# A list of waiting instructions per engine behind a planner, in a one-core hybrid attention and state-space layer

## The chip, the core and the metric

The kernel runs as one program on one core of a Trainium2 chip. A core has a matrix engine (PE, with its weight loads shown as PEld), a vector engine (DVE), a scalar engine (ACT), a general engine (POOL) and a sync engine (SP) that issues most transfers. Each engine works through its own list of instructions in the order in which the program wrote them; an instruction that waits for another engine holds all that stand behind it on its own engine. The metric is the device time of one execution in microseconds (us), the median of several runs.

## What is computed

One layer for 1024 positions of width 2048 in float32: a combined input projection, sparse attention in half of the width, a Mamba-2 state-space mixer in the other half, an output projection and a LayerNorm on the residual.

```
u = einsum('bsd,de->bse', h, w_in)
q, k, v, z_attn, q_idx, k_idx, w_idx, z_ssd, xbc, dt_raw = split(u)
o_attn = dsa_attention(rope(q), rope(k), v, rope(q_idx), rope(k_idx), w_idx) * silu(z_attn)
o_ssd  = ssd_mixer(xbc, z_ssd, dt_raw, ...)
sub = einsum('bse,ed->bsd', concat(o_attn, o_ssd), w_out)
h = layer_norm(alpha * h + sub)
```

In the attention an indexer scores all admissible keys of a query, the 256 best are kept, and softmax attention with 8 query heads over 2 key heads runs on these.

## The kernel before

**Arithmetic.** The two projections run in blocks of 128 by 128 by 512. Each float32 operand is split into a high part and a rest, and three products are added: high by high, high by rest, rest by high. Most of the weight is handled in a Strassen-like scheme of seven products over sums of blocks. Names in the profile: `wr` is a raw piece of weight (128x512), `wh` its high part made by ACT, `wl` the rest made by DVE or POOL; `xh` and `xl` are the same for the activations; `pj`, `a` and `o` are PSUM banks; `u` is the general SBUF tile; `s` (program name `s4`) a wider one; `sm` small columns; `mx`, `pt`, `o_sc` and the like are scratch in DRAM. One piece of weight feeds twelve matmuls of the input projection.

**Stages, roughly.** The span begins with plain projections and the indexer's scores of the first half of the rows (0 to 215 us), goes on with products of the Strassen scheme among state-space and attention work (to 1350 us, with the top-256 search by bisection on ACT and DVE from about 600 us on), and ends with the output projection (from 1350 us) and the LayerNorm.

**What sets the order.** `Layer.run` walks through the pieces of the projections in a fixed order and writes out their matmuls. Between them `Flow.pump` advances some hundred tasks (Python generators such as `t_w` for splitting one piece of weight, `t_x` for an activation, `t_ssd`, `t_attn`, `t_topk`), the first in the list of priorities that is `ready`. What ready means is decided by a model, class `Sim`: it keeps a clock for each engine, a cost for each operation, the times at which data are written, and the port that DVE and POOL share. Every operation passes through `Engine.__getattr__`: it is written into the program at once (`f(*args, **kw)`), and `Sim.run` then advances the model's clocks. So the program's order on each engine is the order in which the planner took the steps, and where two steps interleave badly, an engine waits in that order. `Flow.new` hands out a tile from a numbered slot; the tile framework makes the first user of the new tile wait for the users of the old one.

All work is issued from one line (L346, the call in `Engine.__getattr__`), so rows of the profile tell operations apart by tile names. Rows of the order carry two numbers on a name: the first is the kernel's own count of tiles and is the same before and after, the second is the framework's.

Of the kernel before, what the change touches and what calls it, by code (L numbers as in the profile page):

```python
# [12 lines left out]
AF = mybir.ActivationFunctionType  # L13
ALU = mybir.AluOpType

D = 2048
# [108 lines left out]
class Port:  # L125
# [3 lines left out]
    def __init__(self):  # L129
        self.busy = []  # L130
# [26 lines left out]
def in_dram(x):  # L157
    return "DRAM" in str(x.space)
# [6 lines left out]
class Sim:  # L165


    LAT = 70.0

    def __init__(self):  # L170
        self.clk = dict(PE=0.0, V=0.0, A=0.0, G=0.0, SP=0.0, AQ=0.0, D=0.0)
        self.slot = {}
        self.port = Port()
        self.table = None
        self.recent = []

    @staticmethod
    def region(x):
# [34 lines left out]
    def note(self, notes, end, eng):  # L213
        for s, p0, p1, a, b, w in notes:
            inside = lambda e: e[0] >= p0 and e[1] <= p1 and e[2] >= a and e[3] <= b
            s[2] = [e for e in s[2] if not (inside(e) and (w or (not e[4] and e[6] == eng)))]
            s[2].append((p0, p1, a, b, w, end, eng))

    def last(self, tile):
# [67 lines left out]
    def run(self, eng, op, outs, ins, kw):  # L287

        if op == "dma_start":
            return self.dma(eng, outs[0], ins[0])  # L290
        n = outs[0].free_size()
        at, notes = self.deps(outs, ins, eng)
        busy, took = self.cost(eng, op, outs, ins, kw, n)
        if eng == "A":
            kind = {AF.Silu: "silu", AF.Exp: "exp", AF.Ln: "ln"}.get(kw.get("func"))
            if kind and kind != self.table:
                self.table = kind
                self.clk["A"] += 1283
# [17 lines left out]
        cell = [start + took, start]  # L316
        if eng == "V":
            self.recent = self.recent[-24:] + [cell]
        self.note(notes, cell, eng)
        return cell  # L320

    def dma(self, eng, out, in_):
        q = {"SP": "SP", "A": "AQ", "G": "G"}[eng]
        at, notes = self.deps([out], [in_], "D")
        start = max(self.clk[q], at)
        self.clk[q] = start + (900.0 if eng == "G" else 400.0)
        sb = in_ if in_dram(out) else out
        row = max(sb.ap[-1][1] * 4, 64)
        x = max(start + 400, self.clk["D"])
        self.clk["D"] = x + max(out.size(), in_.size()) * 4 * (1 / 352 + 0.35 / row) * (2.0 if eng == "G" else 1.2 if in_dram(out) and in_dram(in_) else 1.0)  # L330
        cell = [self.clk["D"] + (2000.0 if eng == "G" else 3400.0), start]
        self.note(notes, cell, "D")
        return cell


class Engine:
# [5 lines left out]
    def __getattr__(self, op):  # L342
        f = getattr(self.engine, op)

        def call(*args, **kw):
            f(*args, **kw)  # L346
            is_ap = lambda x: hasattr(x, "tensor") and hasattr(x, "ap")
            outs = [x for x in args[:1] if is_ap(x)] + [kw[k] for k in ("out", "accum_out") if is_ap(kw.get(k))]
            ins = [x for x in args[1:] if is_ap(x)] + [x for k, x in kw.items() if is_ap(x) and k not in ("out", "accum_out")]
            if op == "tensor_tensor_reduce":  # L350
                outs.append(ins.pop())
            if op == "activation" and len(args) > 2:
                kw["func"] = args[2]
            self.flow.placed(self.flow.sim.run(self.name, op, outs, ins, kw))
        return call


# [6 lines left out]
class Event:  # L364
# [5 lines left out]
    @property  # L370
    def t(self):
        return max(c[0] for c in self.cells) if self.cells else None
# [15 lines left out]
class Flow:  # L388
# [6 lines left out]

    def __init__(self, nc):
        self.sim = Sim()
        self.nc = Engines(self, nc)
# [12 lines left out]
    @property  # L411
    def t(self):
        return self.sim.clk["PE"]

    def placed(self, cell):
        self.steps += 1
        self.last = cell
        self.cells.append(cell)
# [8 lines left out]
    def new(self, tag, shape, dtype=F):  # L427

        free = self.slots[tag]
        assert free, ("no slot", tag)  # L430
        slot = min(free)
        free.remove(slot)
        self.n += 1
        home, i = slot[1]
        t = self.pool[home].tile(shape, dtype, name=f"{home}_{self.n}", tag=f"{home}{i}")
        self.where[t.tensor.name] = (tag, slot[1])
        if tag == "u" and self.mixing:
            self.mixed.add(t.tensor.name)
        return t
# [153 lines left out]
class Layer:  # L593
# [316 lines left out]
    def run(self):  # L910
        fl = self.fl
# [1298 lines left out]
```

## Time and profile before

| | |
|---|---|
| median of 3 runs | 1756.56 us (1754.19 to 1759.01) |
| the profiled execution's own time | 1756.95 us |
| its span, first to last instruction | 1754.8 us |
| PE busy | 1642.7 us, 94% |
| DVE busy | 1353.6 us, 77% |
| ACT busy | 985.3 us, 56% |
| POOL busy | 259.9 us, 15% |
| mean granted clock of PE | 0.98 |
| DMA | 431.67 MB, 246 GB/s |

The profile shows one execution. A matmul's duration in it covers its way through the array, and the next one starts before it ends; the pace is read from the starts. Idle time in front of an instruction stands in brackets in the timeline, with what ended it.

### The profile page before, as it was taken

What the parts mean: (1) busy time and instruction counts of PE and PEld (TensorE: products, weight loads), DVE (VectorE), ACT (ScalarE), POOL (GpSimd) and SP (SyncE); (2) the same over time, 40 slices, a digit from 0 to 9 for tenths busy, and PEclk for the clock granted to TensorE, in tenths of its full rate; (3) what the DMA queues carried; (4) which work ended last, traced back from release to release, by engine and by line L of the source; (5) the groups of instructions that cost most, each with busy time, mean ns of one, the idle gap of its engine ahead of it and who ended that gap; (6) DMA issues with size and microseconds to landing.
All of it is one profiled execution on the core that took longest, in us unless ns stands there. A gap on an engine that the chain in (4) does not pass through costs nothing.

```text
span 1754.8 us, 26174 instructions
## 1 busy us (share of the span) xinstructions
PE 1642.7 (94%) x7989; PEld 1344.5 (77%) x7989; DVE 1353.6 (77%) x2991; ACT 985.3 (56%) x1920; POOL 259.9 (15%) x321
## 2 busy tenths in 40 slices
PE   7999999999999899899899999989999889999993
PEld 6888878777777678787677788878788778778782
DVE  6897465568898878888966677898886778888875
ACT  6657766655665498988732456547555434323351
POOL 2200021001112100002131322002111000100122
PEclk9999999999999999999999999999999999999997
DMA  8599888596377688989899897886565997777998
GB/s 290 170 308 349 233 262 230 144 314 156 86 240 214 198 248 277 324 251 294 284 273 313 253 300 193 249 293 203 190 200 173 315 296 242 228 211 237 332 267 199
DMA packets 272685, 431.67 MB, mean 246 GB/s; under 512 B 29600, under 2 KB 87328, under 8 KB 272032
## 3 DMA queue, kind: packets, MB, share of 16 engines
q1 hardware_dynamic: 259872, 406.93, 70.6%
q0 software_dynamic: 12672, 23.07, 8.9%
q8 instruction: 63, 1.03, 0.2%
q14 instruction: 78, 0.64, 0.1%
HBM read 338.56 MB, written 131.17 MB: 268 GB/s over the span
## 4 chain that ended last, share of the span: by engine, by line
PE 53%; DVE 19%; DMA 14%; ACT 6%; issue 5%; SPq 2%; POOL 1%; DVEq 0%; POOLq 0%; ACTq 0%
PE pj L346 40%; DVE u L346 9%; PE a L346 8%; PE o L346 5%; DVE wl L346 3%; ACT u L346 3%; DMA wr<-wt 2%; DMA u<-mx 2%; DVE s L346 2%; DVE xl L346 2%; SPq L346 2%; DVE wr L346 2%; DMA u<-xt 1%; ACT wh L346 1%; DMA u<-arow 1%
## 5 line engine op out<-in xcount | busy, mean ns | idle before, releaser
L346 PE MATMUL pj<-xh,wh 128*128 128x512 f32 (+1 forms) x1520 | 595.7, 392 | 30.1 <-ACT wh L346 26.7
L346 PE MATMUL pj<-xh,wl 128*128 128x512 f32 (+1 forms) x1520 | 586.1, 386 | 19.8 <-DVE wl L346 19.5
L346 PE MATMUL pj<-xl,wh 128*128 128x512 f32 (+1 forms) x1520 | 583.8, 384 | 0.9 <-POOL xl L346 0.6
L346 ACT ACTIVATE wh<-wr 128x512 fp32r<-128x512 f32 (+1 forms) x488 | 298.7, 623 | 283.0 <-PE pj L346 118.8
L346 DVE TENSOR_TENSOR wl<-wr,wh 128x512 fp32r<-128x512 f32 (+1 forms) x456 | 311.3, 693 | 148.2 <-ACT wh L346 145.9
L346 PEld LDWEIGHTS pj<-xh,wh 128*128 128x128 f32 x1520 | 288.1, 190 | 88.7 <-ACT wh L346 32.9
L346 PEld LDWEIGHTS pj<-xh,wl 128*128 128x128 f32 x1520 | 287.8, 189 | 88.0 <-DVE wl L346 32.1
L346 PEld LDWEIGHTS pj<-xl,wh 128*128 128x128 f32 x1520 | 288.6, 190 | 52.2 <-POOL xl L346 1.3
L346 PE MATMUL a<-u,u 128*128 128x512 f32 (+3 forms) x776 | 176.5, 351 | 3.7 <-ACT u L346 1.3
L346 DVE TENSOR_TENSOR u<-u,u 128x512 f32<-128x512 f32 (+6 forms) x240 | 147.3, 626 | 14.3 <-ACT u L346 10.4
L346 PEld LDWEIGHTS a<-u,u 128*128 128x128 f32 x776 | 127.2, 190 | 37.5 <-DVE s L346 9.1
L346 ACT ACTIVATE u<-u 128x512 f32<-128x512 f32 (+4 forms) x209 | 116.1, 576 | 62.3 <-DVE u L346 42.2
L346 ACT ACTIVATE u<-a 128x256 fp32r<-128x256 f32 (+3 forms) x182 | 61.3, 364 | 149.3 <-PE a L346 72.1
L346 ACT ACTIVATE u<-s,sm 128x1024 bf16<-128x1024 f32 (+7 forms) x132 | 129.7, 983 | 19.2 <-DVE sm L346 17.3
L346 PE MATMUL pj<-wh,xh 128*128 128x512 f32 x310 | 128.4, 414 | 4.6 <-ACT xh L346 3.8
L346 DVE TENSOR_TENSOR xl<-u,xh 128x512 fp32r<-128x512 f32 (+1 forms) x168 | 111.1, 693 | 27.9 <-ACT xh L346 27.4
L346 ACT ACTIVATE xh<-u 128x512 fp32r<-128x512 f32 (+1 forms) x184 | 102.4, 586 | 47.6 <-DVE u L346 18.5
L346 DVE TENSOR_TENSOR wr<-wr,wr 128x512 f32<-128x512 f32 x160 | 114.9, 719 | 14.7 <-DMA wr<-wt 11.7
L346 PE MATMUL pj<-wl,xh 128*128 128x512 f32 x310 | 122.9, 396 | 1.1 <-DVE wl L346 1.1
L346 PE MATMUL pj<-wh,xl 128*128 128x512 f32 x310 | 123.0, 397 | 0.9 <-DVE xl L346 0.9
L346 POOL DMA_DIRECT2D o<-wo x64 | 53.1, 843 | 458.9 <-DMA o<-wo 250.4
L346 ACT ACTIVATE a<-a 128x512 f32<-128x512 f32 (+3 forms) x160 | 76.2, 505 | 71.4 <-PE a L346 69.1
(164 smaller groups left out, 2065.3 us busy)
## 6 DMA issues: line engine op xcount, KB each, us to landing
wr<-wt SPq DMA_DIRECT2D x424, 256.0 KB, 5.1
u<-xt SPq DMA_DIRECT2D x80, 256.0 KB, 5.9
u<-mx SPq DMA_DIRECT2D x72, 256.0 KB, 5.5
o<-wo POOLq DMA_DIRECT2D x64, 256.0 KB, 6.5
u<-x SPq DMA_DIRECT2D x64, 256.0 KB, 5.3
wr<-o SPq DMA_DIRECT2D x64, 256.0 KB, 5.0
pt<-u SPq DMA_DIRECT2D x48, 256.0 KB, 3.2
u<-pt SPq DMA_DIRECT2D x48, 256.0 KB, 4.8
```

The source lines that it names most:

```text
L346: f(*args, **kw)
```

## The change

Instructions are no longer written into the program when they are planned. `Engine.__getattr__` now makes a closure `go` and hands it to the new `Flow.call`. That runs the planner's model as before (`Sim.run`, so every decision of the planner is the same), collects the instructions on which the new one depends by its data (`Sim.before`), gives it a cost, and puts it into a list for its engine. The new class `Queue` has clocks of its own and writes the instructions out. Its `step` looks at the first 12 (PE), 10 (DVE, ACT, POOL) or 8 (SP) of each list, takes of each engine the oldest one that is ready when the engine is free, or else the one that will be ready first, and writes out the earliest over all engines. It is run only as far as is needed: `Flow.new` runs it until all users of the slot's old tile are written out, and the end of `Layer.run` empties it. Matmuls into one PSUM tile keep their order, and ACT's functions that need a table keep theirs. This second model has no shared port of DVE and POOL; its transfer time is 4000 ns on SP's queue where the planner's is 3400.

With lists of length one the program on each engine is, row by row, the one before. As it is, 7,450 of 7,675 PE instructions are written out when they are the oldest of their list, 2,009 of 2,869 on DVE, 1,176 of 1,609 on ACT, 292 of 317 on POOL and 1,213 of 1,738 on SP (counted in the program, as are the next numbers). Of 488 splits `wh` on ACT 183 stand earlier among ACT's instructions than before, by 2.3 places on average, and 69 later by 1.7; of 456 splits `wl` on DVE 145 earlier by 2.3 and 96 later by 2.2. Of 184 `xh` on ACT 24 stand earlier and 71 later by 3.1; of 168 `xl` on DVE 18 earlier and 66 later by 3.8. The 49 table loads stay 49.

```diff
     def note(self, notes, end, eng):
...
-            s[2] = [e for e in s[2] if not (inside(e) and (w or (not e[4] and e[6] == eng)))]
+            s[2] = [e for e in s[2] if not (inside(e) and (w or (not e[4] and e[6] == eng and e[5] is not end and e[5][2].end is not None)))]
...
+    def before(self, eng, outs, ins):
+
+        recs, floor = [], 0.0
+        for w, xs in ((False, ins), (True, outs)):
+            for x in xs:
+                k, name, p0, p1, a, b = self.region(x)
+                floor = max(floor, self.floor.get(name, 0.0))
+                s = self.slot.get(k)
+                if s is not None and s[0] == name:
+                    recs += [e[5][2] for e in s[2] if (e[4] or w) and (e[2] < b and a < e[3] and e[0] < p1 and p0 < e[1]
+                                                                       or w and e[6] == eng == "PE")]
+        return recs, floor
...
+class Queue:
...
+    WIN = dict(PE=12, V=10, A=10, G=10, SP=8)
+    LAND = 4000.0
+    LAT = 75.0
...
+    def step(self):
+        best = None
+        for e, q in self.pend.items():
+            free = self.clk[e]
+            if best and free >= best[0]:
+                continue
+            for i, c in enumerate(q[:self.WIN[e]]):
+                at = c.floor
+                for r in c.recs:
+                    if r.end is None:
+                        break
+                    t = r.end + (0.0 if r.eng == e and not r.size else self.LAT) if not r.eng == e == "PE" else 0.0
+                    if t > at:
+                        at = t
+                else:
+                    at = max(at, free)
+                    if best is None or at < best[0]:
+                        best = at, e, i
+                    if at == free:
+                        break
+        at, e, i = best
+        c = self.pend[e].pop(i)
+        c.go()
...
         def call(*args, **kw):
-            f(*args, **kw)
+            go = lambda: f(*args, **given)
+            given = dict(kw)
...
-            self.flow.placed(self.flow.sim.run(self.name, op, outs, ins, kw))
+            self.flow.call(self.name, op, outs, ins, kw, go)
...
+        old = self.sim.users(self.keys.get((home, i)))
+        self.queue.until(old)
         t = self.pool[home].tile(shape, dtype, name=f"{home}_{self.n}", tag=f"{home}{i}")
...
         fl.drain()
+        fl.queue.flush()
```

Two places show what moves. The first is on ACT at about 602 to 612 us of the span. `wh_1328` and its neighbours are high parts of weight, `u_1323<-a_1338` is a copy of the state-space mixer, the rows with 128x640 and 128x1024 are steps of the top-256 search. Before:

```order
L346 ACTIVATE wh_1336_6795<-wr_1249_6367 128x512
L346 ACTIVATE u_1323_6735<-a_1338_6812 128x128
L346 ACTIVATE wh_1339_6819<-wr_1268_6472 128x512
L346 ACTIVATE u_1317_6716,sm_1316_6715<-s4_949_4988,sm_1316_6715 128x640
L346 ACTIVATE u_1317_6716,sm_1316_6715<-s4_952_4991,sm_1316_6715 128x1024
L346 ACTIVATE wh_1328_6742<-wr_1292_6582 128x512
L346 ACTIVATE u_1335_6791,sm_1334_6790<-s4_950_4989,sm_1334_6790 128x768
```

With the change, on the same engine at the same place:

```order
L441 ACTIVATE wh_1336_6777<-wr_1249_6355 128x512
L441 ACTIVATE wh_1328_6724<-wr_1292_6566 128x512
L441 ACTIVATE wh_1339_6798<-wr_1268_6461 128x512
L441 ACTIVATE u_1323_6689<-a_1338_6780 128x128
L441 ACTIVATE u_1323_6689<-a_1346_6808 128x128
L441 ACTIVATE wh_1332_6749<-wr_1306_6654 128x512
L441 ACTIVATE u_1317_6683,sm_1316_6682<-s4_949_4976,sm_1316_6682 128x640
```

`wh_1328` and `wh_1339` have moved in front of the copy, and the two long search steps behind it.

The second place is SP's list at about 1357 to 1366 us, at the start of the output projection: `u_3087<-mx1_6` and `u_3098<-mx1_7` load activations that become `xh` and `xl`, the other `mx` loads are for later products. Before:

```order
L346 DMA u_3087_14913<-mx1_6_284 128x512
L346 DMA u_3088_14918<-hst2_296 128x256
...
L346 DMA u_3095_14928<-arow1_299 128x512
L346 DMA u_3098_14933<-mx1_7_285 128x512
L346 DMA u_3103_14947<-mx1_0_278 128x512
L346 DMA u_3104_14949<-mx0_0_262 128x512
L346 DMA u_3107_14953<-mx1_1_279 128x512
L346 DMA u_3108_14955<-mx0_1_263 128x512
```

With the change:

```order
L441 DMA u_3088_14904<-hst2_217 128x256
...
L441 DMA u_3095_14911<-arow1_220 128x512
L441 DMA u_3103_14945<-mx1_0_199 128x512
L441 DMA u_3104_14946<-mx0_0_183 128x512
L441 DMA u_3107_14949<-mx1_1_200 128x512
L441 DMA u_3108_14950<-mx0_1_184 128x512
L441 DMA u_3087_14903<-mx1_6_205 128x512
L441 DMA u_3098_14914<-mx1_7_206 128x512
```

Four `mx` loads that were behind the two now stand in front of them, and `u_3087` has also gone behind the loads of the state-space step.

## Rows read from the trace of the kernel before

**Rows 1.** The head of the page: the span, and busy time, share and instructions of PE and DVE.

```profile
span 1754.8 us, 26174 instructions
PE 1642.7 (94%) x7989; PEld 1344.5 (77%) x7989; DVE 1353.6 (77%) x2991; ACT 985.3 (56%) x1920; POOL 259.9 (15%) x321
```

**Rows 2.** Busy time by stretch of the span: start:end, length, busy us of PE, PEld, DVE, ACT and POOL (with counts), granted clock of PE, share of DMA, GB/s.

```profile
0.00:50.00 50.00, 40.18 (x237) 33.08 (x238) 34.10 (x71) 28.79 (x65) 13.06 (x25) 0.97 0.87 284
50.00:600.00 550.00, 535.65 (x2563) 438.25 (x2562) 406.86 (x947) 337.87 (x693) 82.89 (x105) 0.99 0.74 224
600.00:900.00 300.00, 275.36 (x1238) 220.52 (x1237) 246.62 (x609) 245.11 (x478) 34.91 (x38) 0.97 0.88 277
900.00:1350.00 450.00, 435.50 (x2210) 362.42 (x2208) 348.82 (x737) 234.91 (x440) 84.28 (x103) 1.00 0.77 239
1350.00:1704.00 354.00, 335.62 (x1661) 273.72 (x1660) 285.31 (x572) 131.21 (x236) 28.45 (x30) 0.98 0.83 264
1704.00:1755.00 51.00, 20.34 (x90) 16.52 (x88) 31.92 (x58) 7.45 (x10) 16.36 (x20) 0.74 0.88 200
```

**Rows 3.** Who PE waited for over the whole span: us in total, times, longest.

```profile
PE pj L346 <- ACT wh L346: 26.7, 11, 8.0
PE pj L346 <- DVE wl L346: 20.6, 23, 4.2
...
PE pj L346 <- ACT xh L346: 5.1, 4, 2.1
```

**Rows 4.** PE's timeline at the longest of these waits: start us, us, operation, count, and in brackets the idle time before it and what ended it.

```profile
612.47 0.80 PE L346 MATMUL pj<-xh,wh 128*128 128x512 f32 x1 [7.96 <-ACT wh L346]
613.06 0.63 PE L346 MATMUL pj<-xl,wh 128*128 128x512 f32 x1
613.49 0.63 PE L346 MATMUL pj<-xh,wl 128*128 128x512 f32 x1
...
616.69 0.39 PE L346 MATMUL pj<-xh,wh 128*128 128x512 f32 x1
616.91 0.39 PE L346 MATMUL pj<-xl,wh 128*128 128x512 f32 x1
```

**Rows 5.** ACT's timeline in the ten microseconds before that matmul, same columns.

```profile
602.03 0.62 ACT L346 ACTIVATE wh<-wr 128x512 fp32r<-128x512 f32 x1
609.02 0.28 ACT L346 ACTIVATE u<-a 128x128 f32<-128x128 f32 x1 [6.37 <-DVE u L346]
609.20 0.62 ACT L346 ACTIVATE wh<-wr 128x512 fp32r<-128x512 f32 x1
609.72 0.82 ACT L346 ACTIVATE u<-s,sm 128x640 bf16<-128x640 int16 x1
...
610.66 1.15 ACT L346 ACTIVATE u<-s,sm 128x1024 bf16<-128x1024 int16 x1
...
611.80 0.61 ACT L346 ACTIVATE wh<-wr 128x512 fp32r<-128x512 f32 x1
```

**Rows 6.** Waits in PE's timeline at seven other places, same columns.

```profile
25.54 0.51 PE L346 MATMUL pj<-xh,wh 128*128 128x256 f32 x1 [3.07 <-ACT wh L346]
...
315.61 1.26 PE L346 MATMUL o<-u,u 128*128 128x256 f32 x3 [2.32 <-ACT u L346]
...
630.04 0.50 PE L346 MATMUL pj<-xh,wh 128*128 128x512 f32 x1 [1.15 <-ACT wh L346]
...
643.76 0.50 PE L346 MATMUL pj<-xh,wh 128*128 128x512 f32 x1 [1.27 <-ACT wh L346]
...
859.72 0.50 PE L346 MATMUL pj<-xh,wh 128*128 128x512 f32 x1 [2.39 <-ACT wh L346]
...
892.37 0.50 PE L346 MATMUL pj<-xh,wh 128*128 128x512 f32 x1 [1.26 <-ACT wh L346]
...
975.04 0.50 PE L346 MATMUL pj<-xh,wh 128*128 128x512 f32 x1 [1.91 <-ACT wh L346]
```

**Rows 7.** Waits in PE's timeline at six more places, same columns.

```profile
740.90 0.79 PE L346 MATMUL pj<-xh,wh 128*128 128x512 f32 x1 [4.49 <-ACT wh L346]
...
1173.58 0.50 PE L346 MATMUL pj<-xh,wh 128*128 128x512 f32 x1 [2.24 <-ACT wh L346]
...
1274.56 0.51 PE L346 MATMUL pj<-xh,wl 128*128 128x512 f32 x1 [4.18 <-DVE wl L346]
...
1365.11 0.50 PE L346 MATMUL pj<-wh,xh 128*128 128x512 f32 x1 [1.69 <-ACT xh L346]
...
1369.32 0.50 PE L346 MATMUL pj<-wh,xh 128*128 128x512 f32 x1 [2.14 <-ACT xh L346]
...
1547.65 0.68 PE L346 MATMUL a<-o,u 128*128 128x1 f32 x4 [3.17 <-DVE u L346]
```

**Rows 8.** SP's timeline at the second place: when it issues the `mx` loads.

```profile
1357.17 0.38 SPq L346 DMA_DIRECT2D u<-mx  x1
...
1363.07 2.85 SPq L346 DMA_DIRECT2D u<-mx  x5
```

**Rows 9.** Who DVE waited for longest over the whole span: us in total, times, longest.

```profile
DVE wl L346 <- ACT wh L346: 145.9, 109, 4.3
```

**Rows 10.** DVE's timeline at one of its longest splits.

```profile
1435.57 1.34 DVE L346 TENSOR_TENSOR wl<-wr,wh 128x512 fp32r<-128x512 f32 x1 [1.44 <-ACT wh L346]
1436.84 0.68 DVE L346 TENSOR_TENSOR s<-o,s 128x512 f32<-128x512 f32 x1
```

**Rows 11.** POOL's timeline at the same time.

```profile
1435.10 1.27 POOL L346 TENSOR_TENSOR xl<-u,xh 128x512 fp32r<-128x512 f32 x1 [11.70 <-ACT xh L346]
```

More of the change, by code (lines that the diff above doesn't have):

```diff
@@ L175, in __init__ @@
         self.recent = []
+        self.floor = {}
     @staticmethod
@@ L215, in note, with users @@
             inside = lambda e: e[0] >= p0 and e[1] <= p1 and e[2] >= a and e[3] <= b
-            s[2] = [e for e in s[2] if not (inside(e) and (w or (not e[4] and e[6] == eng)))]
+            s[2] = [e for e in s[2] if not (inside(e) and (w or (not e[4] and e[6] == eng and e[5] is not end and e[5][2].end is not None)))]
             s[2].append((p0, p1, a, b, w, end, eng))
+    def before(self, eng, outs, ins):
[9 more added lines that the diff above has]
+        return recs, floor
+    def users(self, key):
+        s = self.slot.get(key)
+        return [e[5][2] for e in s[2]] if s else []
     def last(self, tile):
@@ L315, in run @@
         self.clk[eng] = start + busy
-        cell = [start + took, start]
+        cell = [start + took, start, None]
         if eng == "V":
@@ L330, in dma, with __init__, put, done @@
         self.clk["D"] = x + max(out.size(), in_.size()) * 4 * (1 / 352 + 0.35 / row) * (2.0 if eng == "G" else 1.2 if in_dram(out) and in_dram(in_) else 1.0)
-        cell = [self.clk["D"] + (2000.0 if eng == "G" else 3400.0), start]
+        cell = [self.clk["D"] + (2000.0 if eng == "G" else 3400.0), start, None]
         self.note(notes, cell, "D")
         return cell
+class Call:
+    __slots__ = ("eng", "go", "recs", "floor", "busy", "took", "size", "table", "end", "cell")
+class Queue:
+    WIN = dict(PE=12, V=10, A=10, G=10, SP=8)
+    LAND = 4000.0
+    LAT = 75.0
+    def __init__(self):
+        self.pend = {e: [] for e in self.WIN}
+        self.clk = {e: 0.0 for e in self.WIN}
+        self.bus = 0.0
+        self.table = self.tabled = None
+    def put(self, c):
+        c.end = None
+        if c.table:
+            if self.tabled is not None:
+                c.recs.append(self.tabled)
+            self.tabled = c
+        self.pend[c.eng].append(c)
+    def step(self):
[21 more added lines that the diff above has]
+        c.go()
+        self.done(c)
+        if c.size:
+            x = max(at + 400, self.bus)
+            self.bus = x + c.size
+            self.clk[e] = at + c.busy
+            c.end = self.bus + (self.LAND if e == "SP" else self.LAND + 500)
+        else:
+            if c.table and c.table != self.table:
+                self.table = c.table
+                at += 1283
+            self.clk[e] = at + c.busy
+            c.end = at + c.took
+        c.go = c.recs = None
+    def done(self, c):
+        pass
+    def until(self, cs):
+        for c in cs:
+            while c.end is None:
+                self.step()
+    def flush(self):
+        while any(self.pend.values()):
+            self.step()
@@ L397, in __init__ @@
         self.sim = Sim()
+        self.queue = Queue()
+        self.keys = {}
         self.nc = Engines(self, nc)
@@ L413, in t, with call @@
         return self.sim.clk["PE"]
+    def call(self, eng, op, outs, ins, kw, go):
+        sim = self.sim
+        c = Call()
+        c.eng, c.go, c.table, c.size = eng, go, None, 0.0
+        c.recs, c.floor = sim.before(eng, outs, ins)
+        if op == "dma_start":
+            d = sim.clk["D"]
+            cell = sim.run(eng, op, outs, ins, kw)
+            sb = ins[0] if in_dram(outs[0]) else outs[0]
+            row = max(sb.ap[-1][1] * 4, 64)
+            c.size = max(outs[0].size(), ins[0].size()) * 4 * (1 / 352 + 0.35 / row) * (
+                2.0 if eng == "G" else 1.2 if in_dram(outs[0]) and in_dram(ins[0]) else 1.0)
+            c.busy, c.took = (900.0 if eng == "G" else 440.0), 0.0
+        else:
+            c.busy, c.took = sim.cost(eng, op, outs, ins, kw, outs[0].free_size())
+            if eng in "VA":
+                c.busy, c.took = c.busy + 20.0, c.took + 20.0
+            if eng == "A":
+                c.table = {AF.Silu: "silu", AF.Exp: "exp", AF.Ln: "ln"}.get(kw.get("func"))
+            cell = sim.run(eng, op, outs, ins, kw)
+        cell[2] = c
+        c.cell = cell
+        self.queue.put(c)
+        self.placed(cell)
     def placed(self, cell):
@@ L434, in new @@
         home, i = slot[1]
+        old = self.sim.users(self.keys.get((home, i)))
+        self.queue.until(old)
         t = self.pool[home].tile(shape, dtype, name=f"{home}_{self.n}", tag=f"{home}{i}")
+        self.keys[home, i] = getattr(t.tensor, "tag", None) or t.tensor.name
+        if old:
+            self.sim.floor[t.tensor.name] = max(c.end + Queue.LAT for c in old)
         self.where[t.tensor.name] = (tag, slot[1])
```

## Prediction, made before the changed kernel was run

> **What bounds the kernel now.** I read the head of the page first. PE is busy 94% of the span, DVE 77% [rows 1]: PE is the bound, and a change that leaves its work alone can only win from the time in which it waits. The table by stretches says how much that is: in the middle, from 50 to 1704 us, PE is busy 535.65 + 275.36 + 435.50 + 335.62 = 1582.1 of 1654 us [rows 2], so 71.9 us are idle. Head and tail hold 9.8 and 30.7 us more; there PE waits for the first loads and for the LayerNorm after the last product, and the order within a list can do little for either. The worst middle stretch is 600 to 900 us, with 24.6 us idle of 300 and ACT busy 245 us.
>
> Next the waits of PE. ACT's high parts of weight `wh` end 26.7 us of them in 11 waits, DVE's rests `wl` 20.6 us in 23, the activations `xh` 5.1 us in 4 [rows 3]. Then why ACT is late. At the longest wait PE stands 7.96 us until 612.47 us [rows 4]. ACT was not short of time: it finished a split at 602.65 us, stood idle 6.37 us at a small copy that waited for DVE, and then took one split and two search steps before the split PE needed, at 611.80 us [rows 5]. Idle and held work together make the wait: a queue blocked at its head. DVE shows the same in small: 145.9 us of its idle time over the span are `wl` waiting for `wh`, in 109 waits of 1.3 us on average [rows 9], with other work behind them.
>
> **The change, part by part.** No matmul, split, transfer or table load is added or removed; a different writer puts the same instructions into the lists. So the sum has no term for work, only for waits that go, waits that come, and the clock.
>
> Waits on ACT that go. In the new order `wh_1328` stands ahead of the blocked copy and the two steps: nothing that held it remains in front except splits of 0.62 us [rows 5]. I count the whole 7.96 us [rows 4]. At the seven other places the instruction PE waits for has also moved in front of what was blocked or working ahead of it on ACT, and by enough to cover the wait or nearly so: 3.07 + 2.32 + 1.15 + 1.27 + 2.39 + 1.26 + 1.91 = 13.4 us [rows 6]. Together 21.3 us.
>
> Waits that stay. At 740.90, 1274.56 and 1547.65 us nothing that matters moves ahead of the late instruction: 4.49 + 4.18 + 3.17 = 11.8 us are left where they are [rows 7].
>
> Waits for DVE's `wl`. Of the 20.6 us [rows 3] about a third by place has its `wl` moved forward, usually past one instruction that is itself 0.68 us long [rows 10]. Bounds: nothing, if the `wh` in front of it is what is late, and 20.6 us, if all of them go. I take 7 us, a third, because the order shows 145 of 456 splits forward.
>
> The clock. After the 7.96 us wait the matmuls start 0.43 us apart, later 0.22 us [rows 4]: the granted clock is at the lower of its levels (1.2 GHz) until it returns to 2.4 GHz, after PE had stood still. From 613.06 to about 616.2 us some seven intervals lose 0.2 us each, 1.4 us. Bounds for all the waits that go: nothing, as after a short one, and as much again per us of wait as here, 1.4 / 7.96 x 28 = 5 us. I take 2 us, since most are short.
>
> Waits that come. On SP's list the loads that become `xh` for 1365.11 and 1369.32 us move behind four other `mx` loads. Five such issues took 2.85 us [rows 8], 0.57 us each, so both are issued about 4 x 0.57 = 2.3 us later. PE waits there already, 1.69 and 2.14 us [rows 7], so this is on its path. But the second load was followed closely by the four, and the same four feed the next products; I charge 2.3 us once. At 1173.58 us the split that PE waits for (2.24 us [rows 7]) has another instruction put in front: 1 us. Elsewhere 69 `wh` move back by 1.7 places and 96 `wl` by 2.2, an instruction there lasting 0.6 to 0.7 us [rows 5, 10]. Their bounds: nothing, if the pieces split ahead and the idle slots filled by the move cover them all, and 69 x 1.7 x 0.62 + 96 x 2.2 x 0.68 = 216 us, if none is covered. Rows that bear on it: of some 944 splits, 34 waits of PE are seen now [rows 3], one in 28; so of 165 moved back some six should be seen, at about 1.4 us each: 8 us. Together 11.3, say 12 us.
>
> SP's queue, 1,738 issues of about 0.4 us [rows 8], puts loads past stores that wait for data; I count that as nothing, hidden by the pieces loaded ahead, since PE's longest waits name splits and not transfers. PE's own order changes in few places, and matmuls of other banks then fill a wait; that is within the 7 us. Tail: DVE's and POOL's last lists keep the same work with swaps of neighbours; nothing.
>
> Sum against the profiled execution: 1756.95 - 21.3 - 7 - 2 + 12 = 1738.65. That execution lies 0.4 us above the median of the three runs, which changes nothing: 1739 us, 1.0% faster.
>
> One thing speaks against trusting the second model. It has no port shared by DVE and POOL. A split of DVE that lasts 0.68 us elsewhere took 1.34 us at 1435.57 us [rows 10] while POOL worked from 1435.10 for 1.27 us [rows 11]. The Trainium skill (SBUF — State Buffer, "Who interferes with whom") says that a DVE instruction with two SBUF inputs contends with a POOL instruction that reads SBUF, and that whichever issues second blocks for the other's whole length; the trace agrees with it here (0.66 us longer). By that rule the new order may put DVE work against POOL's that the planner's model kept apart. Going by rows alone, 0.66 us at each of the 25 places where POOL takes one out of turn would be 16 us of DVE time; DVE is idle 23% [rows 1], so I add nothing to the sum, and leave it to the range.
>
> **The rivals.** *Larger gain.* Filled idle slots add up: what ACT and DVE do in a slot they waste now is not in the way later, so backlogs shrink well beyond the places named. For it speaks that DVE alone wastes 145.9 us at splits [rows 9]; against it that PE can use no more than 71.9 us, and that it is busy 96.8% in 900 to 1350 us, where there is little to win. Half of the idle time gone and 4 us of clock: 1756.95 - 36 - 4 = 1717 us.
>
> *No effect.* PE waits for whichever operand comes last; as one split gets earlier the next one is late, and the 28 us come back at other pieces. For it: the four late activations and the places of rows 7 stay. Time: 1756.95 +/- 5.
>
> *Slower.* The second model takes from each list what it believes ready, and so pays for a fuller engine with the urgent work that was next. The activations are where this bites: 71 of 184 `xh` and 66 of 168 `xl` go back, by 3.1 and 3.8 places, about 2.1 us at 0.62 us a place. PE waits little for `xh` now (5.1 us [rows 3]), so there is room; but if that room is used up, 137 x 2.1 = 288 us of delay are there to be seen. The loss passes the gross gain of 30 us once one in ten of these is seen by PE. At one in six: 48 us, with the gain of 30: 1756.95 + 48 - 30 = 1775 us. It would lie in the stretches with many new activations, 1350 to 1704 us above all. Against it: SP issues many of their loads earlier.
>
> *It doesn't do what it says.* The new order is real on DVE, ACT and SP, as the counts show, but on PE 7,450 of 7,675 keep their turn; this case gives the time of no effect and is counted there.
>
> **How the numbers follow.** A measurement of this kernel can tell about 0.3% from no change, 5.3 us, so faster means below 1751.3. The forecast gets 0.47 (own range 1726 to 1750), the larger gain 0.18, no effect 0.13, slower 0.22. Faster: 0.47 + 0.18 = 0.65; same 0.13; slower 0.22. For 8 in 10 the low end reaches past the larger gain's 1717 to 1712, and the high end to 1768, which leaves out the worst part of the slower case.
>
> **What would show it.** Right: at about 600 us no ACT wait of six microseconds in front of the small copy and PE's wait of 8 us gone; PE's waits for `wh` down from 26.7 to about 8 us, those for `wl` to about 14; DVE's idle at `wl` for `wh` far below 145.9 us; PE's busy time in the middle about unchanged while the middle is some 18 us shorter. Wrong in size: the table by stretches with 600 to 900 us still at 275 of 300. Wrong in sign: waits of PE for `xh` or `xl` of over 25 us, or DVE instructions next to POOL's grown long by tens of microseconds in sum.

## The result, and the profile after

| | before | with the change |
|---|---|---|
| median | 1757.01 us (1754.19 to 1759.01) | 1680.84 us (1679.39 to 1681.48) |
| ratio | | 0.9566 [0.955, 0.9583] |
| span | 1754.8 us | 1677.6 us |

The change gains 4.3%, 76 us. The prediction had the sign and missed the size: 1739 us was forecast, and the range ended at 1712.

The head of the page after, which answers to [rows 1]:

```profile
span 1677.6 us, 26207 instructions
PE 1613.9 (96%) x7989; PEld 1342.0 (80%) x7989; DVE 1345.1 (80%) x2991; ACT 985.6 (59%) x1920; POOL 273.9 (16%) x321
```

The span is 77.2 us shorter. PE's idle time fell from 1754.8 - 1642.7 = 112.1 to 1677.6 - 1613.9 = 63.7 us, which gives 48.4. The other 28.8 us are busy time, with the same 7,989 matmuls. So PE's busy time before also held time that was lost; the part on the prediction takes it apart.

The table by stretches after, for [rows 2]; the columns are the same:

```profile
0.00:50.00 50.00, 44.95 (x270) 38.64 (x271) 38.58 (x77) 31.30 (x69) 13.38 (x26) 0.93 0.89 295
50.00:1650.00 1600.00, 1568.61 (x7721) 1303.39 (x7720) 1291.84 (x2889) 951.22 (x1847) 252.24 (x287) 1.00 0.83 257
1650.00:1678.00 28.00, 0.30 (x2) 0.00 (x0) 14.67 (x26) 3.04 (x4) 8.30 (x10) 0.56 0.85 183
```

In the middle 31.4 of 1600 us are idle, against 71.9 of 1654. Even the first 50 us hold 4.8 us more of PE's work.

Who waited for whom after, over the whole span (us, times, longest), for [rows 3] and [rows 9]:

```profile
DVE wl L441 <- ACT wh L441: 113.1, 108, 3.9
...
PE pj L441 <- DVE wl L441: 10.3, 13, 3.0
...
PE pj L441 <- ACT wh L441: 5.1, 2, 5.0
...
PE pj L441 <- ACT xh L441: 4.6, 2, 3.4
```

PE's waits for `wh` fell from 26.7 to 5.1 us, those for `wl` from 20.6 to 10.3, and DVE's for `wh` from 145.9 to 113.1.

The same place as [rows 4] and [rows 5], now near 582 us. ACT's timeline after:

```profile
579.62 0.63 ACT L441 ACTIVATE wh<-wr 128x512 fp32r<-128x512 f32 x1 [0.36 <-DVE wr L441]
581.35 0.63 ACT L441 ACTIVATE wh<-wr 128x512 fp32r<-128x512 f32 x1 [1.09 <-PE pj L441]
581.90 0.28 ACT L441 ACTIVATE u<-a 128x128 f32<-128x128 f32 x1
582.70 0.28 ACT L441 ACTIVATE u<-a 128x128 f32<-128x128 f32 x1 [0.52 <-PE a L441]
582.88 0.62 ACT L441 ACTIVATE wh<-wr 128x512 fp32r<-128x512 f32 x1
583.39 0.82 ACT L441 ACTIVATE u<-s,sm 128x640 bf16<-128x640 int16 x1
```

PE's timeline after, same place:

```profile
585.61 0.80 PE L441 MATMUL pj<-xh,wl 128*128 128x512 f32 x1 [2.95 <-DVE wl L441]
586.21 0.63 PE L441 MATMUL pj<-xh,wh 128*128 128x512 f32 x1
586.63 0.63 PE L441 MATMUL pj<-xl,wh 128*128 128x512 f32 x1
```

DVE's timeline after, same place:

```profile
583.01 0.68 DVE L441 SCALAR_TENSOR_TENSOR u<-pj,u 128x512 f32<-128x512 f32 x1
583.61 0.41 DVE L441 TENSOR_TENSOR u<-a,dt 128x256 f32<-128x256 f32 x1
583.94 0.41 DVE L441 TENSOR_TENSOR u<-a,ddt 128x256 f32<-128x256 f32 x1
584.27 1.28 DVE L441 TENSOR_TENSOR wl<-wr,wh 128x512 fp32r<-128x512 f32 x2
```

The copy with 6.37 us of idle time in front of it is now one with 0.52 us at most, and the `wh` is in time. But PE still waits 2.95 us, for the `wl` of such a piece: DVE works without a gap and has two products in front of it.

The chain of work that ended last (followed back from the last instruction, at each step to what released it), by engine, before:

```profile
PE 53%; DVE 19%; DMA 14%; ACT 6%; issue 5%; SPq 2%; POOL 1%; DVEq 0%; POOLq 0%; ACTq 0%
```

and after:

```profile
PE 72%; DVE 11%; DMA 9%; issue 3%; ACT 2%; POOL 1%; SPq 0%; DVEq 0%; POOLq 0%; ACTq 0%
```

The shares of DVE, DMA and ACT fell by 8, 5 and 4 points and PE's rose by 19. The prediction had looked at ACT above all.

### The profile page after: what moved, and what is told of

The parts are those of the page before. It is cut to its first block, busy times and chain, and to the rows that moved or that the text cites. A ratio compares the mean times of both kernels' runs of the same rounds, so it can differ in the third digit from the quotient of the medians.

```text
span 1677.6 us, 26207 instructions
## 1 busy us (share of the span) xinstructions
PE 1613.9 (96%) x7989; PEld 1342.0 (80%) x7989; DVE 1345.1 (80%) x2991; ACT 985.6 (59%) x1920; POOL 273.9 (16%) x321
## 4 chain that ended last, share of the span: by engine, by line
PE 72%; DVE 11%; DMA 9%; issue 3%; ACT 2%; POOL 1%; SPq 0%; DVEq 0%; POOLq 0%; ACTq 0%
PE pj L441 55%; PE a L441 10%; PE o L441 8%; DVE u L441 4%; DVE wr L441 2%; DVE wl L441 2%; DMA wr<-wt 2%; DMA u<-xt 2%; DVE s L441 1%; ACT u L441 1%; DMA u<-x 1%; DVE xl L441 1%; DMA u<-arow 1%; ACT wh L441 1%; DMA u<-st9s 0%
## 5 line engine op out<-in xcount | busy, mean ns | idle before, releaser
L441 ACT ACTIVATE wh<-wr 128x512 fp32r<-128x512 f32 (+1 forms) x488 | 302.2, 626 | 369.0 <-PE pj L441 175.4
L441 DVE TENSOR_TENSOR wl<-wr,wh 128x512 fp32r<-128x512 f32 (+1 forms) x456 | 317.9, 704 | 118.6 <-ACT wh L441 113.1
L441 DVE TENSOR_TENSOR u<-u,u 128x512 f32<-128x512 f32 (+6 forms) x240 | 151.7, 643 | 4.6 <-ACT u L441 3.0
L441 ACT ACTIVATE u<-s,sm 128x768 bf16<-128x768 int16 (+7 forms) x132 | 129.0, 978 | 21.2 <-DVE sm L441 20.8
```

Of the source, the lines that this page charges most:

```text
L441: go = lambda: f(*args, **given)
```

## The experiments

Each ratio is to runs of the kernel before on the same chip, with its 95% interval. Where only `WIN` differs from the changed kernel, the diff shows the line that stands in its place; a list of length one keeps an engine's order as it was.

**ACT's list alone.**

```diff
-    WIN = dict(PE=12, V=10, A=10, G=10, SP=8)
+    WIN = dict(PE=1, V=1, A=10, G=1, SP=1)
```

> Lists of length one on PE, DVE, POOL and SP, ten on ACT: only ACT's order is freed. Theory N (the named waits: what the prediction counted for ACT, 21.3 us plus 2 us of clock, and nothing that builds up): 1733 to 1736 us. Theory B (idle slots add up: an engine's order alone gives part, and ACT, DVE and SP together far more than the sum of them one by one): 1735 to 1750, and the kernel with both ACT and DVE freed beats the sum of the two by 10 us or more. Theory L (the gain is carried by loads that pass blocked stores on SP): no more than 5 us faster than before, over 1750.

Measured: 1758.93 us, 1.0015 [0.9997, 1.0033], no gain. Only theory L had over 1750 us, and it expected the same of DVE's list, which measured otherwise (next). PE's waits in this kernel:

```profile
PE pj L441 <- DVE wl L441: 42.8, 23, 5.4
...
PE pj L441 <- ACT wh L441: 4.3, 3, 3.0
```

PE's timeline at the place of [rows 4]:

```profile
611.15 0.50 PE L441 MATMUL pj<-xh,wh 128*128 128x512 f32 x1 [0.68 <-ACT wh L441]
...
617.29 0.80 PE L441 MATMUL pj<-xh,wl 128*128 128x512 f32 x1 [5.41 <-DVE wl L441]
```

DVE's timeline there:

```profile
613.53 0.68 DVE L441 SCALAR_TENSOR_TENSOR u<-pj,u 128x512 f32<-128x512 f32 x1
...
614.79 0.68 DVE L441 TENSOR_TENSOR wl<-wr,wh 128x512 fp32r<-128x512 f32 x1
616.20 0.16 DVE L441 TENSOR_TENSOR sm<-sm 128x2 f32<-128x2 f32 x1 [0.73 <-ACT u L441]
...
616.55 0.69 DVE L441 TENSOR_TENSOR wl<-wr,wh 128x512 fp32r<-128x512 f32 x1
```

The `wh` waits go as forecast, 26.7 to 4.3 us, and come back as `wl` waits, 20.6 to 42.8. At this place the early split does not help: its rest is held on DVE by work in the old order, two of the mixer's products and another `wl`, and at the end three small search columns, for which DVE stands 0.73 us, since they wait for the very ACT steps that have moved back.

**DVE's list alone; SP's alone; PE's alone; ACT's and DVE's; DVE's and SP's.**

```diff
-    WIN = dict(PE=12, V=10, A=10, G=10, SP=8)
+    WIN = dict(PE=1, V=10, A=1, G=1, SP=1)
...
+    WIN = dict(PE=1, V=1, A=1, G=1, SP=8)
...
+    WIN = dict(PE=12, V=1, A=1, G=1, SP=1)
...
+    WIN = dict(PE=1, V=10, A=10, G=1, SP=1)
...
+    WIN = dict(PE=1, V=10, A=1, G=1, SP=8)
```

> Ten on DVE, one elsewhere: only DVE's order is freed. Theory N: 7 us for wl, so about 1749. Theory B: 1735 to 1750, with DVE's idle time at wl for wh shorter by at least 20 us of its 145.9. Theory L: over 1750.

> Eight on SP, one elsewhere: only the order of the transfers that SP issues is freed. Theory N, which charged SP's order 2.3 us for four mx loads put ahead and gave it nothing: 1757 to 1762. Theory L: at least 30 us faster, under 1727. Theory B: a small part of the gain by itself, 1740 to 1757, since PE's waits name splits and not transfers.

> Twelve on PE, one elsewhere. If PE's order is worth something by itself (a matmul of another bank fills a wait for a split), it gives the 15 us by which the full change beats the one with PE's list at one: 1738 to 1746. If it is worth something only together with the other lists, as ACT's order turned out to be, it gives 0 to 5 us: 1751 to 1757.

> Ten on ACT and DVE, one on PE, POOL and SP. Theory N: the sum of the two alone, 28 us and 2 us of clock, about 1727. Theory B: below 1715, at least 10 us more than the sum of ACT alone and DVE alone. Theory L: about 1750, as the transfers stay in the old order.

> Ten on DVE and eight on SP, one on PE, ACT and POOL. Additive: 31 us of DVE alone and 30 us of SP alone, 1693 to 1699. Theory O (the same waits): 1703 to 1715. If ACT's order counts once DVE's is free, this stays at least 10 us behind the full change's 1681.

Measured: DVE alone 1726.08 us, 0.9818 [0.978, 0.9856]; SP alone 1726.8, 0.9832 [0.98, 0.9864]; PE alone 1722.65, 0.9807 [0.9792, 0.9821]; ACT and DVE 1720.31, 0.9801 [0.9767, 0.9834]; DVE and SP 1708.5, 0.9721 [0.9694, 0.9747]. DVE's and PE's times lie below every stretch expected for them, SP's just inside theory L's, that of ACT and DVE between those of N and B; only DVE and SP together came out as one of theirs had it, O's. Three engines gained about 30 us each by themselves, and the three would make more than the whole. That called for a control, below: it shows that most of each 30 us is one and the same part, which does not need a freed list at all. Against that control none of the three gains more than the intervals allow.

**All lists but SP's; all but PE's; all but ACT's.**

```diff
-    WIN = dict(PE=12, V=10, A=10, G=10, SP=8)
+    WIN = dict(PE=12, V=10, A=10, G=10, SP=1)
...
+    WIN = dict(PE=1, V=10, A=10, G=10, SP=8)
...
+    WIN = dict(PE=12, V=10, A=1, G=10, SP=8)
```

> Lists of full length on PE, DVE, ACT and POOL, one on SP. Theory S (SP's order is a part of its own: its 30 us come on top of the others'): 76 - 30 us of gain, 1708 to 1714. Theory O (the orders remove the same waits: where one engine's head is free the others' gain less): much of SP's gain is covered, 1685 to 1700.

> Full length on DVE, ACT, POOL and SP, one on PE. If matmuls that pass a late one are a part of the gain (225 of 7,675 are written out of turn), this loses it: at one interval of 0.23 us to 1 us for each of the 225 passes, 5 to 25 us, so 1686 to 1706. If PE's order only follows, 1679 to 1684.

> The full change with ACT's list of length one, all others as they are. ACT's order alone stood 1.6% behind the lists of length one (1.0015 against 0.9856). If ACT's order is bad as such, this kernel is faster than the full change: about 1655 to 1675 us. If it is bad only while DVE keeps its order (the splits wh then come earlier than wl can follow), it is needed here: 1690 to 1715 us.

Measured: without SP 1702.66 us, 0.9692 [0.9659, 0.9725]; without PE 1696.2, 0.9649 [0.9622, 0.9675]; without ACT 1688.26, 0.9608 [0.9586, 0.9631]. Against the full change, SP's list is worth 22 us beside the others, PE's 15 and ACT's 7. The run without SP lies between the stretches of its two theories, the one without PE in the first of its two, the one without ACT a little below its second: ACT's order is of use once DVE can follow. Without it PE waits for `wh` again; PE's waits in that kernel:

```profile
PE pj L441 <- ACT wh L441: 15.8, 10, 4.2
PE pj L441 <- DVE wl L441: 5.6, 14, 0.8
```

What SP's list does beside the others stands in the waits of ACT and DVE that a transfer ended: summed over the whole table of waits they are 60.9 us without SP's list and 30.6 with it. Two of these groups, without it:

```profile
ACT xh L441 <- DMA u<-mx: 6.2, 7, 1.4
...
DVE wr L441 <- DMA wr<-wt: 6.0, 5, 2.9
```

and in the changed kernel:

```profile
ACT xh L441 <- DMA u<-mx: 1.3, 2, 1.0
...
DVE wr L441 <- DMA wr<-wt: 0.4, 2, 0.2
```

All lists but DVE's was not run.

**What SP gains by.** SP's list alone, and only instructions that store to DRAM and are not ready may be passed.

```diff
+                if e == "SP" and not c.store:
+                    break
...
+        c.store = in_dram(outs[0])
```

> As the run with SP's list alone at eight, but a transfer may pass only stores that are not ready (a transfer into DRAM waits for its data), and never a load that waits for its slot. If loads that stand behind blocked stores make SP's 30 us: 1724 to 1732. If it is loads that wait for a slot or for data in DRAM and hold other loads: 1745 to 1757.

Measured: 1721.5 us, 0.9801 [0.9786, 0.9815], no less than SP's whole order (0.9832 [0.98, 0.9864]), and inside the first of the two stretches but for 3 us. It does not show what the first theory says, though: the control below, with no list freed, is at 0.9856 [0.9815, 0.9897], so most of these 35 us are not SP's. What the waits show is that passing stores does for them what the whole order does: those of ACT and DVE that a transfer ended add up to 93 us in the control, 58 with SP's list at eight and 51 here. Whether SP's 22 us beside the other lists are that too was not run.

**Longer lists; the planner's own numbers; a shared port.** Lists of 20 to 24 (16 on SP); the second model with the planner's transfer time and without its own additions; the second model with the planner's port of DVE and POOL.

```diff
+    WIN = dict(PE=24, V=20, A=20, G=20, SP=16)
...
+    LAND = 3400.0
+    LAT = 70.0
...
+                    if c.port:
+                        at = self.port.take("V", at, max(c.busy - 20, 10))[0]
```

> Twice the window on every engine. If what is left of the waits is still order (a ready instruction that stands just outside the window), faster than the change by 5 us or more, under 1676. If the lists rarely reach their end (index 9 of ten is chosen 5 times on DVE and ACT each), within 5 us of 1681. If passing over more than ten puts urgent splits back: over 1686.

> The full change with the planner's own numbers in the second model: 3400 and 2000 ns for a transfer to land in place of 4000 and 4500, 400 ns for an issue on SP in place of 440, no 20 ns more on DVE and ACT, a latency of 70 in place of 75 ns. If the rule of the oldest ready one makes the gain: within 8 us of 1681. If the closer numbers make it: over 1700.

> The full change with the planner's shared port of DVE and POOL in the second model too. If DVE instructions that meet POOL's cost time on PE's path, as the slower case in the prediction weighed: 5 us or more faster than 1681. If they only take idle time of DVE: within 4 us of it.

Measured: 1679.1 us, 0.9554 [0.9529, 0.9578]; 1682.23, 0.9574 [0.9557, 0.959]; 1684.51, 0.9592 [0.9576, 0.9608]. All three intervals overlap that of the change, and each time lies in the stretch of the theory by which the edit matters little. Neither these numbers nor a longer list decides; lists between one and the change's length were not run. A model that knows the port is not better. The Trainium skill (SBUF — State Buffer, "Who interferes with whom"), cited ahead as what speaks against the second model, agrees with the 1.34 us split of [rows 10]; in the time of this kernel no run shows a cost of leaving it out.

**The control: all lists of length one.**

```diff
-    WIN = dict(PE=12, V=10, A=10, G=10, SP=8)
+    WIN = dict(PE=1, V=1, A=1, G=1, SP=1)
```

> The changed kernel with every list of length one: the rows on every engine are those of the kernel before, in the same order, but they are written out by the second model, which crosses the engines in another sequence, so that some waits between engines differ (of two engines that read one PSUM tile, the later written waits for the earlier). Theory 'order': what gains is the order within the lists alone; then this kernel is the kernel before, 1754 to 1760 us, and ACT's idle time before its small copy stays near 87 us. Theory 'readers': part of the gain comes from ACT's small copy that no longer waits for DVE's two products from the same PSUM tile; then 1720 to 1735 us, with ACT's idle time before that copy near 27 us, although no row has changed its place. In that case the orders of DVE, SP and PE alone, each about 30 us faster than before, were worth almost nothing by themselves, and ACT's order alone lost some 30 us.

Measured: 1730.96 us, 0.9856 [0.9815, 0.9897], as theory 'readers' had it. A third of the gain comes although no row has changed its place on its engine. What has changed is which of two engines waits. The mixer's step reads one PSUM tile three times: DVE's two products take columns 0 to 256, ACT's small copy takes 256 to 384. Of two engines that read one tile, the later written waits for the earlier. Before, DVE's products are always written first; the second model, in which reads don't wait for reads, writes 25 of the 32 copies first (counted in the program; the same 25 with SP's or PE's list alone, 24 in the changed kernel). The groups of these instructions (busy us, mean ns, idle time before and what ended it), before:

```profile
L346 DVE TENSOR_TENSOR u<-a,dt 128x256 f32<-128x256 f32 x32 | 13.4, 417 | 5.0 <-PE a L346 5.0
...
L346 ACT ACTIVATE u<-a 128x128 f32<-128x128 f32 x32 | 8.8, 276 | 87.3 <-DVE u L346 63.1 <-PE a L346 14.4 <-DVE sm L346 9.6
```

and with lists of length one:

```profile
L441 DVE TENSOR_TENSOR u<-a,dt 128x256 f32<-128x256 f32 x32 | 13.4, 418 | 5.2 <-PE a L441 5.0 <-ACT u L441 0.2
...
L441 ACT ACTIVATE u<-a 128x128 f32<-128x128 f32 x32 | 8.6, 272 | 26.5 <-PE a L441 24.7 <-DVE u L441 1.4
```

ACT's 63.1 us behind DVE are all but gone, and DVE pays 0.2. PE's waits in the control, which are what a single freed list has to be held against:

```profile
PE pj L441 <- ACT wh L441: 21.9, 9, 5.4
PE pj L441 <- DVE wl L441: 19.5, 23, 3.1
```

The Trainium skill (PSUM — Partial Sum Buffer, "PSUM bank collisions raise a hardware error") gives a reason for such a wait: two engines that read the same bank and quadrant at once collide, also in disjoint columns, so it can be turned round but not left out. The rows show the wait; a collision no run here shows.

**That wait turned round in the kernel before, everywhere and at the 25 places.** First the copy ahead of the products in all 32 steps; then only where the lists of length one do it.

```diff
+                fl.act(bn[:, k, 0:128], b[:, 256:384])
                 fl.tt("V", v4(xdt[:, k]), v4(b[:, 0:256]), bc(sd["dt"], c), ALU.mult)
                 fl.tt("V", v4(xdd[:, k]), v4(b[:, 0:256]), bc(sd["ddt"], c), ALU.mult)
-                fl.act(bn[:, k, 0:128], b[:, 256:384])
...
+                late = self.nth in (1, 2, 5, 7, 13, 22, 24)
+                if not late:
+                    fl.act(bn[:, k, 0:128], b[:, 256:384])
...
+                if late:
+                    fl.act(bn[:, k, 0:128], b[:, 256:384])
```

> The kernel before, with one edit: ACT's small copy out of the PSUM tile is written ahead of DVE's two products that read the same tile, no list changed. Theory 'order': 1754 to 1760 us. Theory 'readers': DVE's product waits for the copy instead of the copy for the products; ACT's idle time before the copy falls from 87 to about 27 us, and the time is that of the lists of length one within 5 us, 1720 to 1735 us; if it gains less than those, other pairs of readers matter as well.

> The kernel before, with ACT's small copy written ahead of DVE's two products at 25 of the 32 places, those at which the lists of length one do so, and behind them at the other seven. If these 25 waits are all of the gain of the lists of length one: their time within 5 us, 1724 to 1736 us, and DVE's idle time at the product below 6 us (14.7 us with all 32 turned round). If not: 1740 us or more, and something else in the deferred writing gains.

Measured: all 32, 1744.18 us, 0.9925 [0.9897, 0.9952]; the 25, 1731.39, 0.9865 [0.9841, 0.989]. The groups with all 32:

```profile
L346 DVE TENSOR_TENSOR u<-a,dt 128x256 f32<-128x256 f32 x32 | 13.4, 420 | 14.7 <-ACT u L346 14.7
...
L346 ACT ACTIVATE u<-a 128x128 f32<-128x128 f32 x32 | 8.5, 269 | 26.0 <-PE a L346 26.0
```

and with the 25:

```profile
L346 DVE TENSOR_TENSOR u<-a,dt 128x256 f32<-128x256 f32 x32 | 13.4, 419 | 5.2 <-PE a L346 5.0 <-ACT u L346 0.2
...
L346 ACT ACTIVATE u<-a 128x128 f32<-128x128 f32 x32 | 8.6, 272 | 25.6 <-PE a L346 24.0 <-DVE u L346 1.4
```

Within the intervals the 25 waits are all of the control's gain, by hand and with no second model. With the copy in front at the other seven places too DVE stands 14.7 us, and the ratio is 0.006 worse, some 10 us; the first expectation, 1720 to 1735 us, missed by that. It took other pairs of readers to be the reason in this case; the second run shows that it is these seven places.

**The wait put back into the full change.** The first edit keeps the planner's order of readers where their columns overlap, the second on the whole tile.

```diff
-                    recs += [e[5][2] for e in s[2] if (e[4] or w) and ...
+                    recs += [e[5][2] for e in s[2] if (e[4] or w or in_psum(x)) and ...
...
+                    recs += [e[5][2] for e in s[2] if in_psum(x) and e[6] != eng]
```

> The full change, except that the second model keeps the planner's order also among instructions that read one PSUM tile, so that ACT's copy is again written behind DVE's products. Theory 'order': within 5 us of the full change, 1676 to 1686 us. Theory 'readers': some 20 to 30 us of the gain go, 1700 to 1712 us, and ACT's idle time before the small copy rises from 26 us towards the 87 us of before.

> The full change, except that the second model keeps the planner's order among all instructions of two engines on one PSUM tile, whatever columns they read (the previous edit of this kind compared columns, and the copy reads other columns than the products, so it touched nothing): 31 of the 32 small copies on ACT are again written behind DVE's products. If the waits between readers are a separate part that adds to the order's gain, the full change loses the 1.4% that lists of length one gained: 1700 to 1712 us. If a queue that may pass the blocked copy doesn't mind it, since other splits go in front, it loses little: 1680 to 1690 us, with ACT's idle time before the copy well below the 87 us of before.

Measured: 1680.96 us, 0.9567 [0.9529, 0.9606], and 1677.61, 0.9548 [0.9526, 0.9571]. The first tells nothing: the copy and the products read other columns, so that it does not bind them, and 23 of the 32 copies still stand first. The second puts all 32 behind the products (counted in the program; the expectation says 31) and loses nothing. The copy's group in it:

```profile
L442 ACT ACTIVATE u<-a 128x128 f32<-128x128 f32 x32 | 8.7, 273 | 23.3 <-DVE u L442 15.4 <-PE pj L442 2.9 <-PE o L442 2.3
```

A list that may pass the blocked copy leaves 15.4 us of ACT's 63.1: at the place of [rows 5] three splits and three search steps now stand on ACT between `wh_1336` and the copy, which followed it directly before (read from the program's order). So the turned wait, worth 25 us by itself, is not a separate part of the 76; the longer lists cover it.

## Why the prediction was wrong in size

The step that failed is the form of the sum: it priced single waits of PE, one by one, and put what the other lists do at nothing or almost nothing. Measured, SP's list is worth 22 us where the sum has 0 and PE's 15 where it has a part of 7, the 12 us of new waits did not come, and 28.8 of the 77.2 us of span are no idle time that the profile shows. Term by term:

**"Waits on ACT that go ... I count the whole 7.96 us", together 21.3.** The waits went, by 26.7 - 5.1 = 21.6 us, but the count as gain failed. At that very place 2.95 us are left as a wait for `wl`, and ACT's order by itself gained nothing: PE needs the rest after the high part, and at the place looked at DVE could not give it. That 21.6 is so near to 21.3 says nothing for the count: with ACT's list alone 22.4 us of these waits went as well, and no time was won. Beside the other lists ACT's is worth 7 us.

**"Waits for DVE's `wl`", 7 us.** 20.6 to 10.3: 10.3 us, about the right size.

**"Waits that come", 12 us.** This charge did not come. At the `mx` loads 1.69 + 2.14 us became one wait of 3.45, without the 2.3 us; `xh` waits in all went from 5.1 to 4.6. Before, ACT waited there 0.96 and 1.04 us for the two loads; now it waits for a sum on DVE and then takes four `xh` in a row:

```profile
1314.55 2.41 ACT L441 ACTIVATE xh<-u 128x512 fp32r<-128x512 f32 x4 [1.93 <-DVE u L441]
```

The splits that moved back elsewhere cost PE nothing that shows in these rows.

**"Waits that stay", 11.8 us.** One of three did. PE's two longest waits after, in its timeline:

```profile
710.31 0.79 PE L441 MATMUL pj<-xh,wh 128*128 128x512 f32 x1 [4.96 <-ACT wh L441]
...
1315.75 0.80 PE L441 MATMUL pj<-wh,xh 128*128 128x512 f32 x1 [3.45 <-ACT xh L441]
```

They answer to 740.90 and to 1365.11 and 1369.32 us of [rows 7]. No wait above 1.1 us is left between them, and none above 0.8 us behind them, so those of 1173.58 and 1274.56 us went, and that of 1547.65 too. So from "nothing that matters moves ahead" at a place it does not follow that its wait stays; that these were backlogs from further up fits, but no run singles it out.

**"SP's queue ... I count that as nothing"** and **PE's order "is within the 7 us".** SP's list is worth 22 us beside the others and PE's 15. "PE's longest waits name splits and not transfers" was the wrong ground: a split can be late because its load is. The waits of ACT and DVE that a transfer ended show it, 60.9 us without SP's list and 30.6 with it. By itself SP's list shortens them too, from 93 to 58 us, and gains nothing clear of the intervals.

**"The clock", 2 us, at most 5.** Worked out from the granted clock over the time to the last matmul, 44.4 us stood at the lower level before and 20.5 after; matmuls of 512 and 256 columns lost 16.4 us at it before and 8.5 after. So some 7.9 us, four times the term.

**The pool of 71.9 us.** The prediction let PE win only from idle time, and held against the larger gain that "PE can use no more than 71.9 us". The gain was 76. Measured from start to start, matmuls of 512 and 256 columns exceeded their usual 0.227 and 0.120 us by 62.4 us of idle time, 16.4 at the lower clock, and 55.0 that are neither before; by 22.2, 8.5 and 39.9 after. The third term, 15.1 us of the gain, is hidden under the matmul in front: a matmul lasts 0.39 us and the next can start 0.22 us after it [rows 4], so the first 0.17 us of a late start leave no gap, and the profile calls PE busy. About half of it is the hidden beginning of waits that show; the other half stands where no gap shows, and that this too is waiting is an inference. The three terms make 63.2 of the 77.2 us; the other 14 lie behind smaller matmuls and in the tail. One of PE's longest groups shows that it is not the single matmul that got shorter (busy us, mean ns, idle time before). Before:

```profile
L346 PE MATMUL pj<-xh,wl 128*128 128x512 f32 (+1 forms) x1520 | 586.1, 386 | 19.8 <-DVE wl L346 19.5
```

After:

```profile
L441 PE MATMUL pj<-xh,wl 128*128 128x512 f32 (+1 forms) x1520 | 585.1, 385 | 10.1 <-DVE wl L441 10.1
```

**"The sum has no term for work, only for waits".** True, but the text ahead took lists of length one for the program before because its rows are the same. Its waits are not, and that alone is 25 to 29 us, though within the full change it is no part of its own. This wait stood in [rows 5] as 6.37 us behind DVE, and what had to be asked of it was why a copy waits for DVE at all.

**The rivals.** The larger gain had the mechanism, that filled slots add up, and at 1717 us still too small a size. Against lists of length one (0.9856), DVE, SP and PE alone gain 0.4, 0.2 and 0.5 per cent of the time before, not beyond the intervals, and ACT loses 1.6; all together gain 2.9. The reading that fits is that an instruction which is early on one engine helps only if the next engine may take it early; the trace with ACT's list alone shows it at one place. The slower case asked for PE waits for `xh` above 25 us; they are 4.6. Of the signs of being right, PE's waits for splits fell as named or further, but PE's busy time did not stay about unchanged: it fell by 28.8 us.

What stays open: what DVE's list is worth beside all others, how the 28.8 us of busy time share out between lists, and why ACT's list alone loses 1.6 per cent against the control, beyond the `wl` waits that it brings.

## What to carry to other kernels

Before summing single waits, run the new order's writer with its freedom taken away: here that control, with not one row moved, was a third of the gain, and against the kernel before every "one engine alone" read some 25 us too good. An order loosened on one engine of a chain of producers can merely move the wait to the next (here, against the control, 21.9 to 4.3 us for `wh` and 19.5 to 42.8 for `wl`), so cost such a change for the chain, and take the bound from the distance of starts, not from idle time. Where two engines read one PSUM tile, look at which of them is written first.

## What was not expected of the hardware

A wait's price in clock did not go with its length. After 7.96 us [rows 4] matmuls start 0.43 us apart for some 3.7 us, after 2.95 us for 3.1 and after 4.96 us for 4.8. After 4.18 us at 1274.56 [rows 7] the first matmul still took 0.51 us, but then they too start 0.43 us apart, and the granted clock from 1275 to 1278 us is 0.50 (1.2 GHz). Two waits of nearly one length in the kernel before differ: after 2.15 us at 509.68 the matmuls slow down, after 2.24 us at 1173.58 [rows 7] they don't, and the granted clock from 1174 to 1177 us is 1.00.

```profile
509.68 0.50 PE L346 MATMUL pj<-xh,wl 128*128 128x512 f32 x1 [2.15 <-DVE wl L346]
...
510.58 0.63 PE L346 MATMUL pj<-xh,wl 128*128 128x512 f32 x1
...
1173.91 0.40 PE L346 MATMUL pj<-xl,wh 128*128 128x512 f32 x1
...
1275.29 0.63 PE L346 MATMUL pj<-xl,wh 128*128 128x512 f32 x1
1275.72 0.63 PE L346 MATMUL pj<-xh,wl 128*128 128x512 f32 x1
```

So each of these waits paid about one price or none, and the forecast's "as much again per us of wait" had no ground.
